# A hybrid attention layer on one core: where eight row-sum pieces, a fifth tile, halved branch loads and an FFN copy stand in the order

## The chip, the cores and the metric

The kernel runs on one core of a Trainium2 chip. A core has TensorE (PE, matmuls and transposes), VectorE (DVE), ScalarE (ACT), GpSimd (POOL) and SyncE (SP), which here only issues DMAs. Each engine works through its own queue in order. The metric is the time of one execution in device microseconds, the median of several runs.

## The reference

One encoder layer on 1024 tokens of width 1024, float32:

```python
h = rms_norm(x, norm_mix)
q_a,k_a,v_a, q_b,k_b,v_b, g_a,g_b = split(h @ w_in)
o_a = neighbourhood_attention(rms_norm(q_a), rms_norm(k_a), v_a, rpb)   # 8 heads of 64
o_b = sliding_window_attention(rms_norm(q_b), rms_norm(k_b), v_b, sink, t5)  # 8 heads, 2 kv heads
y = sigmoid(g_a) * (o_a @ w_branch_a) + sigmoid(g_b) * (o_b @ w_branch_b)
x = x + y @ w_out
h = rms_norm(x, norm_ffn)
x = x + (silu(h @ w_gate) * (h @ w_up)) @ w_down          # hidden width 2816
```

## The kernel before

**Numbers in two parts.** Every float32 operand of a large product is held as a high part (a cast) and a low part (what the cast left out); a product is three matmuls, high x high, high x low, low x high. The helper `split` does this everywhere: its cast on ACT has line L61 (L64 with a scale), its subtraction on DVE line L62 (L65 with a scale). In names, `h` and `l` behind a weight (`wb10h`, `wb10l`) are these parts, `ph` and `pl` those of a transposed tile of probabilities. The large products after the attention combine 2 x 2 blocks in seven products instead of eight; they need sums of blocks of weights (L863, class `Seven`) and of blocks of token rows (`row_sums`, class `TokenSums`).

**Order.** The PE's order is written out by hand. DVE, ACT, POOL and SP have an order that a scheduler makes from dependences, priorities and program order; `tc.issue_after(ins)` keeps what is issued inside it behind `ins`, and in the FFN's first part ACT and DVE are scheduled by hand (`change`).

**Attention.** Six head groups (`gi` 0 to 5, kind `na` or `sw`) are projected by `projection`. Each of eight token tiles gives a bank `pj` (24 matmuls, L328). Then `squares` takes the row norms of q and k (a square on ACT, the reduction L339 on DVE, an addition L343 and a power L347 on POOL), `values_out` writes the values (L368 on DVE), `scalings` applies the norms (L375). After tiles 3 and 7 `layout` transposes keys and queries in blocks: keys into a bank `tk`, scaled into `k` (L294 and L295), queries into `tq` (transposes L301, scaled by L280). `keys` and `pair` go through `both`. The tile after tile 3 is the fifth, tile 4, and its squares and values come while the first blocks of keys and queries are still in work.

The scores of a head go block by block (`scores`): two matmuls (L640, L641) into `s`, then DVE adds the bias and takes the minimum (L646), ACT takes the exponential (L652), DVE the reciprocal (L653), POOL multiplies (L654). Three steps later `flip` transposes the tiles (L664, into `tp`) and splits them (`ph`, `pl`), two steps later `values` multiplies by the values (L698). Between these, `filler` feeds PE other work at a planned rate: the projections of later groups, then gate products (`plain_gate`, L465 to L467, scaled on DVE by L491). During the gate products the row sums of the later stage are made: `row_sums` is a generator of eight pieces per index j, for the lines L539 and L540 (t1), a split (put 5), L544 (t2), put 6, L548 (t3), put 7, L552 (t4) and put 4. In `step`, piece n of j = 0 is issued at product step 26 + n, of j = 1 at 40 + n, each behind the last bound instruction (`att["bound"]`, a score sum L646 or a low half `pl`).

**Gates and branches.** Then `gate_pair` (d = 2 to 7) runs the seven products of the gate weights, into banks X, Y, V and Z (L881 to L883); it adds banks (L946, L950) and scales them (L930) on their way to DRAM. `prefetch` loads what comes two steps on, weights or, from d = 8, `load_branch`: one DMA of 128 x 1024 for the two branches' weights (`wb0s` for d = 0), then a split of each half behind the chain of earlier splits (`in_chain`). PE's product `bankX` (weights `g_1l` of gate 7) follows in that chain. The branch products then use the weights and the stored gates (`sg`).

**FFN.** After the output product the FFN's first two hidden blocks (generators `ga`, `gb`) take their seven products in the order `LAST2`; a bank is copied by L885 and L1409 on ACT, fed operands come from `feed`, weights from `prepare_ffn`, sums of weights from `add_up_ffn`. `ffn_norm` makes the second norm: transposes L1277, a reduction L1279 and a scaling L1280 on DVE, a power L1281 on POOL; `spread_norm` spreads it with transposes (L169).

Of the kernel before, what the change touches and what calls it, by code (L numbers as in the profile page):

```python
# [36 lines left out]
def block_kernel(ctx, tc, x, xt, small, w_qkv, w_gates, rpb, t5, w_branch, w_out, w_gate, w_up, w_down,  # L37
# [160 lines left out]
    class GroupWeights:  # L198
# [13 lines left out]

        def split(self, k):
            hi, lo = w_hi(f"wg{self.gi}_{k}"), w_lo(f"wg{self.gi}_{k}")
            split(hi[:, :384], lo[:, :384], self.st[k // 2][:, k % 2, :], nc.gpsimd if k % 2 and self.gi > 1 else nc.vector)
            self.his.append(hi)
            self.los.append(lo)

# [19 lines left out]
    def projection(gi, weights, pending, after=None):  # L238
# [17 lines left out]
        def both(parts):  # L256

            if gi:
                for part in parts:
                    part()()  # L260
            else:
                for low in [part() for part in parts]:
                    low()
# [67 lines left out]
        def squares(tiles):  # L331

            n, t0 = len(tiles), tiles[0][0]
            ss = ap.tile([P, 16], F32, tag="ss", name=f"ss{gi}_{t0}", bufs=4)[:, :n * nh]
            norms = ss.rearrange("p (t h) -> p t h", h=nh)
            for i, (t, ps) in enumerate(tiles):
                qn = ap.tile([P, 320], F32, tag="qn", name=f"qn{gi}_{t}", bufs=7)
                nc.scalar.activation(qn[:, :nqk], ps[:, :nqk], AF.Square)
                nc.vector.tensor_reduce(norms[:, i], qn[:, :nqk].rearrange("p (h e) -> p h e", e=HD),  # L339
                                        axis=AX.X, op=ALU.add)  # L340
                qns.append(qn)
            if n == 1:
                nc.gpsimd.tensor_scalar(ss, ss, 1.0, rows_eps[:, t0:t0 + 1], op0=ALU.mult, op1=ALU.add)  # L343
            else:
                nc.gpsimd.tensor_tensor(norms, norms, rows_eps[:, t0:t0 + n].unsqueeze(2).to_broadcast([P, n, nh]),
                                        ALU.add)
            nc.gpsimd.tensor_tensor(ss, ss, mhalf[:, :n * nh], ALU.pow)  # L347
            return tiles, norms

        def values_out(tiles):  # L350

            for t, ps in tiles:
                rs = rows_rs[:, t:t + 1]
                if kind == "na":
                    for j in range(nk):
                        nc.scalar.activation(v[j][:, t, 0, :], ps[:, nqk + j * HD:nqk + j * HD + HD], AF.Copy, scale=rs)
                else:
                    vs = ap.tile([P, HD], F32, tag="vs", name=f"vs{gi}_{t}", bufs=2)
                    nc.scalar.activation(vs, ps[:, nqk:384], AF.Copy, scale=rs)
                    dst = vnat[idx * T + t * 8:idx * T + t * 8 + 1, :]  # L360
                    nc.sync.dma_start(bass.AP(dst.tensor, dst.offset, [[64 * HD, 16], [HD, 8], [1, HD]]), vs)
                    if t == 7:
                        vr = slot_v(f"vr{gi}")[:, :512].rearrange("p (b e) -> p b e", e=HD)
                        nc.sync.dma_start(vr, vnat[idx * T:(idx + 1) * T, :].rearrange("(b p) e -> p b e", p=P))
                        late_v.append(vr)
            for t, ps in tiles if kind == "na" else ():
                for j in range(nk):
                    nc.vector.scalar_tensor_tensor(v[j][:, t, 1, :], ps[:, nqk + j * HD:nqk + j * HD + HD],  # L368
                                                   rows_rs[:, t:t + 1], f(v[j][:, t, 0, :]),
                                                   op0=ALU.mult, op1=ALU.subtract)  # L370

        def scalings(tiles, norms):

# [107 lines left out]
    def plain_gate(d, br, wg, step=None, room=()):  # L481

        for half in range(2):
# [7 lines left out]
            nc.vector.tensor_mul(raw, pg, wide_rs[half])  # L491
            nc.sync.dma_start(gate_rows(d, br, half), raw)

    def filler(pending):
        for gi in range(1, len(order)):
            for i, cost in enumerate(projection(gi, weights[gi], pending, weights.get(gi + 1))):
                if gi == len(order) - 1 and i == 58:
                    wg = gate_weights(1, 0)
                yield cost
        todo = [(0, 1), (1, 1), (0, 0), (1, 0)]  # L500
        for i, (d, br) in enumerate(todo[:3]):
            def step(half, k):
                if i == 0 and not half and k in (1, 4):
                    wide_norm(k // 4, bank("pj", f"wide{k}"))
                if (i, half, k) == (1, 0, 0):
                    load_pair(0, slot_v, dma)
                at_step = 16 * i + 8 * half + k
                if at_step == 32:
                    load_pair(1, slot_v, dma)
                if at_step in range(26, 34) or at_step in range(40, 48):  # L510
                    if at_step in (26, 40):
                        j = at_step // 40
                        g22 = early.setdefault("g22", slot_u("g22h") if not j else None)
                        early[j] = row_sums(j, halves(g22)[j])
                    with tc.issue_after(att["bound"]):
                        next(early[at_step // 40])
                if (half, k) == (0, 7):
                    step.next = gate_weights(*todo[i + 1][::-1])
                if (half, k) in ((0, 6), (1, 3), (2, 1)):
                    pop(pending)  # L520
            yield from plain_gate(d, br, wg, step)
            wg = step.next
        last_gate.append(wg)
# [46 lines left out]
    with tc.tile_pool(name="at", bufs=1) as ap:  # L570
# [165 lines left out]
        for j in range(4):  # L736
            load_x(1, j)
        for k in range(8):
            if k % 2:
                weights[0].split(k)  # L740
                feature(k, 0)
            else:
                feature(k, 0)
                weights[0].split(k)
# [26 lines left out]
        for g in range(n + LP):  # L771
            before = plan[g - 1] if g else due[0]
            if g < n:
                hd, qb = steps[g]
                while hd["gi"] not in ready:
                    fill(done_chunks[1] + 1)
                if g == 0:
                    opening.close()
                scores(hd, qb)
                if qb == 1 and g + 8 < n:  # L780
                    load_bias(steps[g + 8][0])
                if qb == (4 if g + 16 >= n else 6) and g + 8 - qb < n:
                    steps[g + 8 - qb][0]["bias"] = bias_table(steps[g + 8 - qb][0])
# [217 lines left out]

    def load_branch(d):
        st = w_stage(f"wb{d}")
        dma(st, w_branch[tok(d), :])
        for br in (1, 0):
            hi, lo = w_hi(f"wb{br}{d}"), w_lo(f"wb{br}{d}")
            in_chain(hi, lo, st[:, half_cols(br)])
# [434 lines left out]
    for i, g in enumerate((ga, gb)):  # L1442
        prepare_ffn((i, 7))
        next(g)
    add_up_ffn(4)
    feed(*((3, j) for j in range(4)))
    for i, g in enumerate((ga, gb)):
        prepare_ffn((i, 3))
        next(g)
    rs = [ffn_norm(half, sets[half]["V"]) for half in range(2)]  # L1450
    feed(*((4, j) for j in range(4)))
    both_blocks()
    prepare_ffn((0, 2), (1, 2))
# [153 lines left out]
```

## Time and profile before

| what | value |
|---|---|
| median of 3 runs | 1306.93 us (1306.88 to 1307.44) |
| the profiled execution | 1306.69 us |
| its span, first to last instruction | 1304.8 us |
| granted TensorE clock | 1.00 |
| instructions | 19431 |
| DMA packets | 88582, 191.91 MB |

The profile gives for each engine when an instruction began, how long it took and what it waited for. A timeline row has the start and length in us, the engine, the line, the operation, the tiles (out<-in), their shape and type, the count, and in brackets the idle time before it with its releaser. A wait row has the engine, its line, what it waited for, us in total, times, and the longest. A window row has the stretch, its length, then the busy time of PE, PEld (weight load), DVE, ACT and POOL with the count of instructions, the granted clock, the busy share of the DMA engines and the GB/s that they moved.

### The profile page before, as it was taken

What the parts mean: (1) busy time and instruction counts of PE and PEld (TensorE: products, weight loads), DVE (VectorE), ACT (ScalarE), POOL (GpSimd) and SP (SyncE); (2) the same over time, 40 slices, a digit from 0 to 9 for tenths busy, and PEclk for the clock granted to TensorE, in tenths of its full rate; (3) what the DMA queues carried; (4) which work ended last, traced back from release to release, by engine and by line L of the source; (5) the groups of instructions that cost most, each with busy time, mean ns of one, the idle gap of its engine ahead of it and who ended that gap; (6) DMA issues with size and microseconds to landing.
All of it is one profiled execution on the core that took longest, in us unless ns stands there. A gap on an engine that the chain in (4) does not pass through costs nothing.

```text
span 1304.8 us, 19431 instructions
## 1 busy us (share of the span) xinstructions
PE 1296.7 (99%) x6583; PEld 1129.2 (87%) x6583; DVE 1017.5 (78%) x2028; ACT 693.9 (53%) x1460; POOL 181.1 (14%) x321
## 2 busy tenths in 40 slices
PE   9999999999999999999999999999999999999998
PEld 9999999999888888888888888888888888888887
DVE  6778867776678758869899878888777799797774
ACT  7677857776654224545556544443444465363531
POOL 1355655464310000000000000000000000000000
PEclk9999999999999999999999999999999999999999
DMA  9432413242434348555763433223323356671532
GB/s 354 108 106 49 121 50 109 62 136 84 140 130 169 114 161 297 195 211 201 261 241 126 154 105 121 105 89 106 105 89 113 122 193 209 248 237 65 188 127 81
DMA packets 88582, 191.91 MB, mean 147 GB/s; under 512 B 16114, under 2 KB 18418, under 8 KB 88482
## 3 DMA queue, kind: packets, MB, share of 16 engines
q1 hardware_dynamic: 88338, 190.65, 43.6%
q8 instruction: 52, 0.85, 0.3%
q14 instruction: 48, 0.39, 0.1%
q10 hardware_dynamic: 144, 0.01, 0.0%
HBM read 133.19 MB, written 52.37 MB: 142 GB/s over the span
## 4 chain that ended last, share of the span: by engine, by line
PE 94%; DVE 2%; POOL 1%; DMA 1%; ACT 1%; issue 1%; SPq 0%; POOLq 0%; ACTq 0%; DVEq 0%
PE pj L328 14%; PE bankZ L881 6%; PE bankZ L882 6%; PE bankZ L883 6%; PE bankY L881 6%; PE bankY L882 6%; PE bankY L883 6%; PE bankX L883 5%; PE bankX L881 5%; PE bankX L882 4%; PE o L698 3%; PE bankV L881 3%; PE bankV L882 3%; PE bankV L883 3%; PE tp L664 3%; PE pb L465 2%
## 5 line engine op out<-in xcount | busy, mean ns | idle before, releaser
L652 ACT ACTIVATE E<-E,nm 128x384 f32<-128x384 f32 (+3 forms) x128 | 75.7, 592 | 49.5 <-DVE nm L646 43.9
L654 POOL TENSOR_SCALAR E<-E,nm 128x384 f32<-128x384 f32 (+1 forms) x128 | 73.4, 574 | 93.1 <-DVE nm L653 73.5
L62 DVE TENSOR_TENSOR pl<-tp,ph 128x384 fp32r<-128x384 f32 (+1 forms) x128 | 66.4, 519 | 18.2 <-ACT ph L61 17.3
L61 ACT CAST ph<-tp 128x384 fp32r<-128x384 f32 (+1 forms) x128 | 57.4, 448 | 21.5 <-PE tp L664 21.0
L61 ACT CAST f<-f 128x512 fp32r<-128x512 f32 x87 | 50.9, 621 | 27.9 <-DMA f<-u_dram 27.6
L62 DVE TENSOR_TENSOR f<-f 128x512 fp32r<-128x512 f32 x87 | 56.2, 685 | 9.5 <-ACT f L61 9.4
L664 PE MATMUL tp<-ident,E 128*128 128x128 f32 x352 | 59.6, 272 | 0.9 <-POOL E L654 0.9
L664 PEld LDWEIGHTS tp<-ident,E 128*128 128x128 f32 x352 | 45.2, 140 | 5.8 <-POOL E L654 1.2
L347 POOL TENSOR_TENSOR ss<-ss,mhalf 128x4 f32<-128x4 f32 (+2 forms) x42 | 49.7, 1183 | 3.0
L698 PE MATMUL o<-pl,v 128*128 128x256 f32 (+2 forms) x160 | 48.9, 306 | 0.5 <-DVE pl L62 0.2
L653 DVE RECIPROCAL nm<-nm 128x1 f32<-128x1 f32 x128 | 20.4, 160 | 37.1 <-ACT E L652 35.9
L1281 POOL TENSOR_TENSOR rs<-rs,mhalf 128x4 f32<-128x4 f32 x2 | 2.2, 1106 | 317.7 <-DVE rs L1280 317.7
L640 PE MATMUL s<-k,q 128*128 128x384 f32 (+1 forms) x128 | 46.0, 359 | 0.0
L698 PE MATMUL o<-ph,v 128*128 128x256 f32 (+2 forms) x160 | 45.8, 300 | 0.0
L641 PE MATMUL s<-k,q 128*128 128x384 f32 (+1 forms) x128 | 41.3, 323 | 0.0
L646 DVE CUSTOM_DVE_ANT_0 E<-s,bsw,cols 128x384 f32<-128x384 f32 (+1 forms) x64 | 37.0, 578 | 5.0 <-PE s L641 4.1
L1291 ACT ACTIVATE u<-u 128x512 f32<-128x512 f32 x44 | 27.5, 629 | 23.0 <-DVE u L1290 21.9
L646 DVE CUSTOM_DVE_ANT_0 E<-s,bna 128x384 f32<-128x384 f32 (+1 forms) x64 | 32.9, 517 | 3.3 <-PE s L641 2.7
L881 PE MATMUL bankZ<-f,f_7h 128*128 128x512 f32 x88 | 34.3, 390 | 0.1
L881 PE MATMUL bankY<-f,f_6h 128*128 128x512 f32 x88 | 34.5, 392 | 0.0
L882 PE MATMUL bankV<-f,f_5h 128*128 128x512 f32 x88 | 34.4, 391 | 0.0
L881 PE MATMUL bankV<-f,f_5h 128*128 128x512 f32 x88 | 34.4, 391 | 0.0
(1256 smaller groups left out, 4608.3 us busy)
## 6 DMA issues: line engine op xcount, KB each, us to landing
f<-u_dram SPq DMA_DIRECT2D x77, 256.0 KB
wg_s<-in_w_gate_dram SPq DMA_DIRECT2D x22, 512.0 KB
u_dram<-u SPq DMA_DIRECT2D x33, 256.0 KB
o_dram<-of SPq DMA_DIRECT2D x32, 256.0 KB
o<-o_dram SPq DMA_DIRECT2D x32, 256.0 KB
sg<-g_dram SPq DMA_DIRECT2D x32, 256.0 KB
g_dram<-go SPq DMA_DIRECT2D x24, 256.0 KB
u_dram<-tau SPq DMA_DIRECT2D x22, 256.0 KB
```

Source lines behind the costliest of these rows:

```text
L61: a = nc.scalar.copy(hi, src)
L62: b = (eng or nc.vector).tensor_tensor(lo, src, f(hi), ALU.subtract)
L328: nc.tensor.matmul(ps[:, :384], (lh, lh, ll)[n], (his, los, his)[n][k][:, :384], start=(k == 0 and n == 0), stop=(k == 7 and n == 2))
L347: nc.gpsimd.tensor_tensor(ss, ss, mhalf[:, :n * nh], ALU.pow)
L646: att["bound"] = nc.vector.tensor_tensor_reduce(E[:, :n], s[:, :n], hd["bias"](qb), -1.0, sk if sw else 1e30, ALU.add, ALU.min, nm[:, 0:1] ...
L652: nc.scalar.activation(E[:, :m], E[:, :m], AF.Exp, bias=nm[:, 0:1], scale=-1.0, accum_out=nm[:, 1:2])
L654: nc.gpsimd.tensor_scalar(E[:, :n], E[:, :n], nm[:, 1:2], 1.0, op0=ALU.mult, op1=ALU.mult)
L664: nc.tensor.transpose(tp[:, tok(j)], hd["E"][qq][:, ko:ko + P], ident)
L698: nc.tensor.matmul(hd["O"][half][:, (a - half * 4) * P:(z + 1 - half * 4) * P], v[:, kb].rearrange("p a e -> p (a e)"), pp[:, (a - q0) * P ...
L881: nc.tensor.matmul(ps, hi[:, tok(j)], bh, start=first, stop=False, skip_group_check=True)
L882: nc.tensor.matmul(ps, hi[:, tok(j)], bl, start=False, stop=False, skip_group_check=True)
L883: nc.tensor.matmul(ps, lo[:, tok(j)], bh, start=False, stop=end, skip_group_check=True)
```

## The change

It has five parts; the computation and the order of PE's matmuls stay.

1. At the start the first weight tile `wg_0` is split on DVE alone, ahead of the first feature tile.
2. In `na` groups (from the second group on) `squares` and `values_out` of tile 4 are issued behind the last split of the key and query blocks issued so far (`att["split"]`).
3. The pieces of the row sums of j = 0 leave the product steps 26 to 33. They go into a list, and `sum_piece`, called behind each `scores`, issues one. What is left is issued when the pieces of j = 1 begin.
4. A branch's load is two DMAs of 128 x 512, that for branch 1 first.
5. In the FFN `ga` goes one product further ahead of the next operands, `gb` follows after the first two of them, and the norm is taken ahead of the other two and of the weights 3.

```diff
@@ split, class GroupWeights
-            split(hi[:, :384], lo[:, :384], self.st[k // 2][:, k % 2, :], nc.gpsimd if k % 2 and self.gi > 1 else nc.vector)
+            src = self.st[k // 2][:, k % 2, :]
+            if self.gi == k == 0:
+                nc.vector.tensor_copy(hi[:, :384], src)
+                nc.vector.tensor_tensor(lo[:, :384], src, f(hi[:, :384]), ALU.subtract)
+            else:
+                split(hi[:, :384], lo[:, :384], src, nc.gpsimd if k % 2 and self.gi > 1 else nc.vector)
@@ both
-                    part()()
+                    att["split"] = part()().ins
@@ squares
+            behind = ExitStack()
+            if n == 1 and t0 == 4 and kind == "na":
+                behind.enter_context(tc.issue_after(att["split"]))
...
+            behind.close()
@@ values_out
+            behind = ExitStack()
+            if len(tiles) == 1 and tiles[0][0] == 4 and kind == "na":
+                behind.enter_context(tc.issue_after(att["split"]))
...
+            behind.close()
@@ ahead of filler
+    row_pieces = []
+
+    def sum_piece():
+        if row_pieces:
+            with tc.issue_after(att["bound"]):
+                next(row_pieces.pop())
@@ step
-                    with tc.issue_after(att["bound"]):
-                        next(early[at_step // 40])
+                    if at_step < 40:
+                        row_pieces.append(early[0])
+                    else:
+                        while row_pieces:
+                            sum_piece()
+                        with tc.issue_after(att["bound"]):
+                            next(early[1])
@@ the start
-            if k % 2:
+            if k % 2 or not k:
                 weights[0].split(k)
                 feature(k, 0)
@@ the loop over steps
                 scores(hd, qb)
+                sum_piece()
@@ load_branch
-        dma(st, w_branch[tok(d), :])
+        for br in (1, 0):
+            dma(st[:, half_cols(br)], w_branch[tok(d), half_cols(br)])
@@ the FFN's first two blocks
         next(g)
+    next(ga)
     add_up_ffn(4)
-    feed(*((3, j) for j in range(4)))
-    for i, g in enumerate((ga, gb)):
-        prepare_ffn((i, 3))
-        next(g)
+    feed((3, 0), (3, 1))
+    next(gb)
     rs = [ffn_norm(half, sets[half]["V"]) for half in range(2)]
+    feed((3, 2), (3, 3))
+    prepare_ffn((0, 3), (1, 3))
```

How this moves instructions is seen at three places. Line numbers in the changed kernel are higher: L300 is the L295 of before, L347 the L339, L380 the L368, L671 the L646, L678 the L653, L504 the L491, L577 the L552, L956 the L930, L972 the L946, L976 the L950, L889 the L863.

DVE in the sixth group, from the score sum E_0_5 on (k_1 is the second key scaling, ss_4 the reduction of the fifth tile, v_0 and v_1 its values), before:

```order
L646 ISA E_0_5_4470,nm_0_5_4471<-s_0_5_4467,bna_4021 128x384
L646 ISA nm_0_5_4471 128x1
L339 TENSOR_REDUCE ss_4_4476<-qn_4_4477 128x4
L368 SCALAR_TENSOR_TENSOR v_0_3965<-pj_4_4398,rows_rs,v_0_3965 128x64
L368 SCALAR_TENSOR_TENSOR v_1_3966<-pj_4_4398,rows_rs,v_1_3966 128x64
L295 SCALAR_TENSOR_TENSOR k_1_3968<-tk_0_4443,cols,k_1_3968 64x512
L653 RECIPROCAL nm_0_5_4471<-nm_0_5_4471 128x1
```

And in the changed kernel:

```order
L671 ISA E_0_5_4470,nm_0_5_4471<-s_0_5_4467,bna_4021 128x384
L671 ISA nm_0_5_4471 128x1
L300 SCALAR_TENSOR_TENSOR k_1_3968<-tk_0_4443,cols,k_1_3968 64x512
L347 TENSOR_REDUCE ss_4_4476<-qn_4_4477 128x4
L380 SCALAR_TENSOR_TENSOR v_0_3965<-pj_4_4398,rows_rs,v_0_3965 128x64
L380 SCALAR_TENSOR_TENSOR v_1_3966<-pj_4_4398,rows_rs,v_1_3966 128x64
L678 RECIPROCAL nm_0_5_4471<-nm_0_5_4471 128x1
```

The key scaling now stands ahead of the fifth tile's reduction and values.

DVE between the score sums E_1_2 and E_1_3 of the last head, in the gate products (hs, ta and tb are tiles of the row-sum pieces), before:

```order
L646 ISA E_1_2_5219,nm_1_2_5220<-s_1_2_5216,bna_4968 128x384
L646 ISA nm_1_2_5220 128x1
L62 TENSOR_TENSOR hs_0_5228<-tb_5134,hs_0_5228 128x512
L491 TENSOR_TENSOR graw_1_1_5245<-pg_1_1_5092,wide_rs_109 128x512
L62 TENSOR_TENSOR wg_0l<-wg01s,wg_0h 128x512
L62 TENSOR_TENSOR pl_0_6_5213<-tp_0_6_5208,ph_0_6_5212 128x384
L62 TENSOR_TENSOR wg_1l<-wg01s,wg_1h 128x512
L653 RECIPROCAL nm_1_2_5220<-nm_1_2_5220 128x1
L62 TENSOR_TENSOR pl_0_7_5242<-tp_0_7_5238,ph_0_7_5241 128x256
L552 SCALAR_TENSOR_TENSOR tb_5134<-xo_4948,cols,ta_5133 128x512
L646 ISA E_1_3_5260,nm_1_3_5261<-s_1_3_5257,bna_4968 128x384
```

And in the changed kernel:

```order
L671 ISA E_1_2_5215,nm_1_2_5216<-s_1_2_5212,bna_4968 128x384
L671 ISA nm_1_2_5216 128x1
L62 TENSOR_TENSOR pl_0_6_5209<-tp_0_6_5204,ph_0_6_5208 128x384
L504 TENSOR_TENSOR graw_1_1_5241<-pg_1_1_5092,wide_rs_109 128x512
L62 TENSOR_TENSOR wg_0l<-wg01s,wg_0h 128x512
L62 TENSOR_TENSOR wg_1l<-wg01s,wg_1h 128x512
L62 TENSOR_TENSOR hs_0_5221<-ta_5142,hs_0_5221 128x512
L678 RECIPROCAL nm_1_2_5216<-nm_1_2_5216 128x1
L62 TENSOR_TENSOR pl_0_7_5238<-tp_0_7_5234,ph_0_7_5237 128x256
L671 ISA E_1_3_5255,nm_1_3_5256<-s_1_3_5252,bna_4968 128x384
```

Of the eight pieces seven stood ahead of E_1_3 in DVE's queue before and four do now (t1, put 5, t2, put 6, whose last row is the hs row here); ahead of the low half pl_0_6 it was six and is three, and ahead of pl_1_1, a few rows further on, eight and seven.

DVE at the first branch load (wb10 and wb00 are the halves, ga7s and g_1 gate 7's weights, go_0 a gate on its way out, s1g a weight sum), before:

```order
L930 TENSOR_TENSOR go_1_6186<-gp_6187,wide_rs_109 128x512
L950 TENSOR_TENSOR go_0_6185<-bankY_5487,gp_6187 128x512
L62 TENSOR_TENSOR wb10l<-wb0s,wb10h 128x512
L930 TENSOR_TENSOR go_0_6185<-go_0_6185,wide_rs_109 128x512
L62 TENSOR_TENSOR wb00l<-wb0s,wb00h 128x512
L62 TENSOR_TENSOR g_1l<-ga7s,g_1h 128x512
L863 TENSOR_TENSOR s1g_6125<-gb_6122 128x512
```

And in the changed kernel:

```order
L956 TENSOR_TENSOR go_1_6186<-gp_6187,wide_rs_109 128x512
L62 TENSOR_TENSOR wb10l<-wb0s,wb10h 128x512
L976 TENSOR_TENSOR go_0_6185<-bankY_5487,gp_6187 128x512
L62 TENSOR_TENSOR wb00l<-wb0s,wb00h 128x512
L62 TENSOR_TENSOR g_1l<-ga7s,g_1h 128x512
L889 TENSOR_TENSOR s1g_6125<-gb_6122 128x512
L956 TENSOR_TENSOR go_0_6185<-go_0_6185,wide_rs_109 128x512
```

The gate's sum went behind the first low half, its scaling behind `g_1l` and the weight sum. On SP each branch load is two issues in its old place.

In the FFN, ACT copies bank Y to bank Z (L885) for the first block straight behind the second copy L1409, where before four casts of operands and one of weights stood between, and for the second block behind two of those casts. DVE takes both norm sums (L1279, L1280) ahead of two of the operands' low parts and of the weights' `f_3l`, where before they stood behind all of these.

## The prediction

> **What bounds the kernel now.** The busy shares of the profile's page come first, then the answer on what TensorE (PE) waited for. A PE row's gap understates a loss, since the ends of matmuls are modelled; I count a stop by starts: the interval from one matmul's start to the next, less the interval that the same shape shows where nothing waits.
>
> ```profile
> PE 1296.7 (99%) x6583; PEld 1129.2 (87%) x6583; DVE 1017.5 (78%) x2028; ACT 693.9 (53%) x1460; POOL 181.1 (14%) x321
> ...
> PE tp L664 <- POOL E L654: 0.9, 1, 0.9
> PE tq L301 <- DVE k L295: 0.6, 1, 0.6
> ```
>
> PE is busy for 1296.7 of 1304.8 us, and neither the number nor the order of its matmuls changes. So nothing can be won but stops of PE, a few us in all, and any wait in a new place is a loss. The change touches two of the waits listed there (tp and tq, quoted) and a third that carries its releaser in its own row below (bankX); the others that I sum are too short for that list and are read from starts.
>
> **Fifth tile of a projection.** The DVE (VectorE) rows of the sixth head group, and PE's beside them:
>
> ```profile
> 305.70 0.41 DVE L339 TENSOR_REDUCE ss<-qn 128x4 f32<-128x256 f32 x1
> ...
> 306.53 0.76 DVE L295 SCALAR_TENSOR_TENSOR k<-tk,cols,k 64x512 fp32r<-64x512 f32 x1
> ...
> 305.83 0.49 PE L664 MATMUL tp<-ident,E 128*128 128x128 f32 x3
> 306.08 0.42 PE L328 MATMUL pj<-wg_3h,h 128*128 128x384 f32 x1
> 306.33 0.33 PE L328 MATMUL pj<-wg_3l,h 128*128 128x384 f32 x1
> 306.50 0.34 PE L328 MATMUL pj<-wg_3h,h 128*128 128x384 f32 x1
> 307.43 0.63 PE L301 MATMUL tq<-ident,qn 128*128 128x128 f32 x4 [0.59 <-DVE k L295]
> ```
>
> A 384-wide L328 takes 0.17 from start to start (306.33 to 306.50), so the tq transposes would begin at 306.67; they begin at 307.43: **0.76 lost**. They write a bank that the second key scaling (L295) still reads. The change puts that scaling where the reduction L339 stood, 0.83 sooner (306.53 to 305.70), which ends it at about 306.46: the stop goes, with 0.07 to spare for the signal, so a few hundredths may stay. What is moved behind it is the fifth tile's reduction, its values and POOL's (GpSimd's) norm work, some 0.8 later. At this place nothing near needs them. In the two other na groups that are held back there is no stop to win, and the same move puts POOL's power behind other work. The closest case is the fifth group:
>
> ```profile
> 243.89 1.02 POOL L347 TENSOR_TENSOR ss<-ss,mhalf 128x4 f32<-128x4 f32 x1
> ...
> 245.90 0.58 POOL L654 TENSOR_SCALAR E<-E,nm 128x384 f32<-128x384 f32 x1 [0.73 <-DVE nm L653]
> ...
> 247.47 0.49 PE L664 MATMUL tp<-ident,E 128*128 128x128 f32 x3
> ```
>
> The power may now start later and stand in front of the multiply that ran at 245.90. Worst case, it begins at 245.85: the multiply ends at 246.87 + 0.58 = 247.5, and the third transpose of that group runs at 247.47 + 2 x 0.08 = 247.6. So the cost is 0, hidden by 1.1 us between 246.48 and 247.6; if that cover goes, 0.1 to 0.3 a group. I take 0.
>
> **Row-sum pieces.** Eight DVE pieces (L540, L544, L548, L552 and the splits between) move from eight consecutive product steps to one behind each of eight scores' sums (L646). PE's three stops in that stretch, the windows around it, and DVE's and POOL's rows:
>
> ```profile
> 365.68 0.33 PE L698 MATMUL o<-ph,v 128*128 128x384 f32 x1
> 365.94 0.45 PE L698 MATMUL o<-pl,v 128*128 128x384 f32 x1
> 366.22 0.38 PE L664 MATMUL tp<-ident,E 128*128 128x128 f32 x2
> ...
> 369.80 0.38 PE L664 MATMUL tp<-ident,E 128*128 128x128 f32 x2
> 371.10 0.33 PE L664 MATMUL tp<-ident,E 128*128 128x128 f32 x1 [0.92 <-POOL E L654]
> 371.18 0.48 PE L465 MATMUL pg<-h,wg_1h 128*128 128x512 f32 x1
> ...
> 357.25:370.59 13.34, 12.83 (x73) 10.64 (x71) 13.14 (x38) 9.21 (x25) 2.34 (x6) 1.00 0.40 136
> 370.59:378.00 7.41, 6.91 (x40) 6.03 (x41) 3.98 (x13) 5.51 (x14) 2.66 (x5) 1.00 0.36 130
> ...
> 367.77 0.54 DVE L646 CUSTOM_DVE_ANT_0 E<-s,bna 128x384 f32<-128x384 f32 x1
> ...
> 366.72 0.58 POOL L654 TENSOR_SCALAR E<-E,nm 128x384 f32<-128x384 f32 x1 [3.04 <-PE tp L664]
> ...
> L552 DVE SCALAR_TENSOR_TENSOR tb<-xo,cols,ta x4: 742/748/1047, 366.8 to 410.3; 128x512 f32<-128x512 f32 x4
> ```
>
> The group of three transposes takes 1.38 from its start to the next matmul (369.80 to 371.18), where 0.25 is usual (305.83 to 306.08): **1.13 lost**. The two starts around 365.94 come 0.26 and 0.28 after the ones before, not 0.17: **0.20 lost**. In the windows (columns PE, PEld, DVE, ACT, POOL) DVE works 13.14 of 13.34 us: it is the bound there, and the eight pieces are its surplus. The third transpose waits for the sum E_1_3, which DVE begins at 367.77, 3.33 before the transpose. For no stop that sum must begin 1.13 sooner, by 366.64. Before, seven pieces stand ahead of it; in the changed order four do. Three fewer pieces, at 0.74 (the L552 minimum) each, are 2.2 us; E_1_3 can begin at about 365.6. The low half that the product at 365.94 waits for had six pieces ahead of it and has three. Against that, the pieces are still done later: seven stand ahead of the low half of pl_1_1 at 370.59, where eight did, so DVE is not later there either, and the window behind it has DVE at 3.98 of 7.41, room for the last one. Gain 1.33, bounds 0 (the surplus stays in front of PE) and 1.5 (smaller gaps near 360 go too).
>
> One row speaks against it: L552 usually takes 0.74 to 0.75, but the one at 366.8, beside POOL's multiply at 366.72, took 1.05. A piece beside a multiply costs up to 0.30 more. The Trainium skill's page "SBUF — State Buffer", section "Who interferes with whom", has a rule for it: a VectorE instruction with two SBUF inputs and a GpSimd instruction that reads SBUF exclude each other, and whichever comes second waits in full. The trace agrees in kind: 0.30 longer, where a full wait to 367.30 would have made it 0.50. By the rule, pieces set between score steps, where POOL multiplies, would each lose some, and the sum would keep 0 of this term. By the rows, two or three of eight may meet a multiply, 0.6 to 0.9 against a spare of 1.0 (366.64 less 365.6): I keep the gain and make the other case a rival.
>
> **Branch loads in halves.**
>
> ```profile
> 487.78 0.62 ACT L61 CAST wb10h<-wb0s 128x512 fp32r<-128x512 f32 x1 [4.20 <-DMA wb0s<-in_w_branch_dram]
> ...
> 488.44 0.69 DVE L62 TENSOR_TENSOR wb10l<-wb0s,wb10h 128x512 fp32r<-128x512 f32 x1 [0.29 <-ACT wb10h L61]
> ...
> 490.25 0.69 DVE L62 TENSOR_TENSOR g_1l<-ga7s,g_1h 128x512 fp32r<-128x512 f32 x1
> ...
> 490.20 0.39 PE L882 MATMUL bankX<-h,g_1h 128*128 128x512 f32 x1
> 490.99 0.50 PE L883 MATMUL bankX<-h,g_1l 128*128 128x512 f32 x1 [0.40 <-DVE g_1l L62]
> ...
> 486.50:487.30 0.80, 0.80 (x6) 0.65 (x5) 0.00 (x0) 0.00 (x0) 0.00 (x0) 1.00 0.83 330
> ...
> 491.00:690.00 199.00, 199.00 (x881) 164.81 (x882) 173.43 (x278) 107.06 (x186) 0.00 (x0) 1.00 0.67 237
> ```
>
> The 512 KB load ends at 487.78 and releases a chain: cast, low half, then DVE's queue up to g_1l, which PE wants at 490.20 + 0.24 = 490.44 and gets at 490.99, 0.74 after DVE begins it: 0.55, and about 0.10 more on the next start (as at 690.42 to 690.76 below), **0.65 lost**. At 330 GB/s (last column of the window) 256 KB take 0.8 us, so the first half lands near 487.0. Its chain keeps its steps: wb10l 0.66 after the landing, g_1l three DVE steps of 0.60 behind wb10l. In those steps the sum L950, now queued behind wb10l and its DMA wait, takes the place of the scaling L930, which goes behind g_1l: the length stays, the beginning moves. So wb10l at 487.66, L950 488.26, wb00l 488.86 (its half lands at 487.78 as the whole did, time for its cast), g_1l 489.46, and PE could go on at 490.20, 0.24 before it wants to. With no earlier landing nothing is won: bounds 0 and 0.65, and I take 0.65, since the rate has its own row here. Cost: eight more issues on SP (SyncE), with gate loads queued behind; the last row shows PE at 199.00 of 199 us from there on, so I price them at 0.
>
> **FFN's first copy and norm sums.**
>
> ```profile
> 686.66 0.58 ACT L1409 COPY p<-bankV 128x512 f32<-128x512 f32 x1
> ...
> 689.78 0.59 ACT L885 COPY bankZ<-bankY 128x512 f32<-128x512 f32 x1
> ...
> 689.27 1.03 PE L1277 MATMUL bankV<-ident,wide_rs 128*128 128x128 f32 x8
> 690.42 0.50 PE L881 MATMUL bankZ<-f,f_7h 128*128 128x512 f32 x1
> 690.76 0.40 PE L882 MATMUL bankZ<-f,f_7h 128*128 128x512 f32 x1
> 691.00 0.39 PE L883 MATMUL bankZ<-f,f_7l 128*128 128x512 f32 x1
> ...
> 694.38 2.19 POOL L1281 TENSOR_TENSOR rs<-rs,mhalf 128x4 f32<-128x4 f32 x2 [317.70 <-DVE rs L1280]
> ...
> 696.00 1.28 PE L169 MATMUL bankV<-ident,rs 128*128 128x128 f32 x8
> ```
>
> Eight transposes begin at 689.27; busy 1.03 less the tail of the last leaves the next matmul due at about 690.14. It starts at 690.42, behind the copy into bankZ: 0.28, and the next start is 0.10 late (0.34 against 0.24): **0.38 lost**. The change issues that copy straight behind the one at 686.66, three us sooner, so the stop goes. The eight L169 transposes take 1.28 where L1277's eight take 1.03: **0.25 lost** to the powers on POOL, which end at 696.57. The norm sums stand two low halves and two weight lows sooner on DVE, four times 0.6 = 2.4 us; the stop goes. f_2, f_3 and the lows of f_3's weights come later by the norm sums, two reductions and two short steps on DVE; nothing that PE waits for now reads them before the L169 transposes, so I take 0, and 0.3 as the upper bound, the size of the stops here.
>
> **The start** gives the first weights' cast from ACT (ScalarE) to DVE.
>
> ```profile
> 6.54 0.72 ACT L64 ACTIVATE h<-x,cols 128x512 fp32r<-128x512 f32 x1 [0.56 <-DMA x<-in_xt_dram]
> ```
>
> ACT idles 0.56 for the second x tile, and PE needs what comes of it: a shift of the first matmuls by the 0.5 of a cast, either way, is taken up there. 0.
>
> **Sum.** 0.76 + 1.33 + 0.65 + 0.38 + 0.25 = 3.37, say 3.4. The profiled execution took 1306.69 (span 1304.8 and 1.9 around it), so it becomes 1303.3; the median is 0.24 above that execution, so I forecast **1303.5**. What a measurement can tell from no change is 0.2%, 2.6 us: faster is below 1304.3, slower above 1309.5.
>
> **The rivals.**
> A, the forecast: all five stops go, 1303.5. Chance 0.50.
> B, the half lands less than 0.56 (0.8 less the 0.24 of spare) ahead of the whole, because rows of 2 KB move more slowly than those of 4 KB or other traffic lies between: the bankX stop stays, in part or whole. For: the 330 GB/s include a store. Against: a half cannot be last. 1303.5 + 0.65 = 1304.15. Chance 0.12, half of it below 1304.3.
> C, DVE and POOL exclude each other in the pieces' new places (the rule on the shared port would do that; its page is named above): four or more collisions at 0.30 eat the spare of 1.0, and 1.33 is not won. 1304.8. Chance 0.17.
> D, another wait stands right behind each of the three large ones (the transposes' other operands, the bank's other readers): half of 0.76 + 1.13 + 0.65 stays, 1304.8. Chance 0.11.
> E, slower than before: DVE's surplus is carried past 370. One piece behind every score sum makes each following low half late by a piece, first pl_1_1. It decides when pl_1_1, which PE does not wait for now, comes less than PE's 1.3 sooner and no slack is left of it. Then 1.33 is not won and four lows wait 0.75 each: 1303.5 + 1.33 + 3.0 = 1307.8; if all eight steps do, 1310.8. For: DVE at 13.14 of 13.34. Against: one piece fewer (0.74) ahead of pl_1_1, and 3.4 us idle behind it (7.41 less 3.98). Chance 0.10, half of it above 1309.5.
> Faster: 0.50 + 0.06 = 0.56. Slower: 0.05. Same: the rest, 0.39 (0.06 of B, C, D and half of E). The range runs from 1302.7 (A, the small gaps near 360 won too, and 0.5 for the spread of the runs shown) to 1305.7 (C and D, 1304.8, and 0.9 for their unknown parts, such as the 0.3 of the fifth tile's groups and of f_2 and f_3); E is left out.
>
> **What would show it.** Right: in the list of PE's waits tp, tq and bankX are gone; the tq transposes start 0.17 after the last L328; E_1_3's sum starts more than 1.1 ahead of where it stood relative to PE's transposes; wb10h is cast more than 0.5 before where a whole load would land; the eight L169 take about 1.03. Wrong: a new row in PE's waits, above all `o <- pl` behind 370 or `tp <- POOL E` in the fifth group (both would be E's or the power's doing), pieces of over 1.0 on DVE (C), or ACT idle for wb0s until 487.7 (B).

## The result, and the profile after

The changed kernel takes 1303.35 us (median of 8 runs, 1302.70 to 1304.54), the kernel before 1307.26 (8 runs, 1306.88 to 1308.03). The ratio is 0.9971, 95% interval 0.9960 to 0.9981: 3.9 us faster, with 2.5 to 5.2 inside the interval. The profiled execution took 1304.54 (span 1302.8), the slowest of the eight; why, comes below.

PE's waits in the changed kernel. The three that the change was about (tp, tq, bankX) are gone:

```profile
PE idle L591 <- POOL ident masks.py:199: 1.4, 1, 1.4
PE pj L333 <- ACT wg_2h L61: 0.6, 1, 0.6
PE o L723 <- DVE pl L62: 0.5, 1, 0.5
```

PE's timeline at the places of the prediction, with three more that it did not sum (10.72, 354.60 and 361.06), and DVE's row of the score sum E_1_3:

```profile
10.72 0.79 PE L333 MATMUL pj<-wg_2h,h 128*128 128x384 f32 x3 [0.57 <-ACT wg_2h L61]
...
307.38 0.34 PE L333 MATMUL pj<-wg_3h,h 128*128 128x384 f32 x1
307.60 0.63 PE L306 MATMUL tq<-ident,qn 128*128 128x128 f32 x4
...
354.60 0.44 PE L723 MATMUL o<-ph,v 128*128 128x384 f32 x1
355.53 0.44 PE L723 MATMUL o<-pl,v 128*128 128x384 f32 x1 [0.50 <-DVE pl L62]
...
361.06 0.22 PE L723 MATMUL o<-ph,v 128*128 128x128 f32 x1
361.13 0.33 PE L723 MATMUL o<-pl,v 128*128 128x128 f32 x1
...
366.21 0.33 PE L723 MATMUL o<-ph,v 128*128 128x384 f32 x1
366.39 0.34 PE L723 MATMUL o<-pl,v 128*128 128x384 f32 x1
366.56 0.38 PE L689 MATMUL tp<-ident,E 128*128 128x128 f32 x2
...
370.11 0.49 PE L689 MATMUL tp<-ident,E 128*128 128x128 f32 x3
370.35 0.48 PE L478 MATMUL pg<-h,wg_1h 128*128 128x512 f32 x1
...
366.83 0.54 DVE L671 CUSTOM_DVE_ANT_0 E<-s,bna 128x384 f32<-128x384 f32 x1
...
489.45 0.39 PE L908 MATMUL bankX<-h,g_1h 128*128 128x512 f32 x1
489.68 0.39 PE L909 MATMUL bankX<-h,g_1l 128*128 128x512 f32 x1
489.90 0.39 PE L907 MATMUL bankX<-h,g_1h 128*128 128x512 f32 x1
...
688.06 1.03 PE L1304 MATMUL bankV<-ident,wide_rs 128*128 128x128 f32 x8
688.85 0.48 PE L907 MATMUL bankZ<-f,f_7h 128*128 128x512 f32 x1
689.17 0.39 PE L908 MATMUL bankZ<-f,f_7h 128*128 128x512 f32 x1
...
694.40 1.03 PE L169 MATMUL bankV<-ident,rs 128*128 128x128 f32 x8
695.20 0.47 PE L907 MATMUL bankY<-f,f_3h 128*128 128x512 f32 x1
```

The same places of the kernel before that have not been shown:

```profile
9.52 0.97 PE L328 MATMUL pj<-wg_2h,h 128*128 128x384 f32 x4
...
354.35 0.34 PE L698 MATMUL o<-ph,v 128*128 128x384 f32 x1
354.75 0.44 PE L698 MATMUL o<-pl,v 128*128 128x384 f32 x1
...
360.27 0.22 PE L698 MATMUL o<-ph,v 128*128 128x128 f32 x1
360.59 0.33 PE L698 MATMUL o<-pl,v 128*128 128x128 f32 x1
...
697.03 0.48 PE L881 MATMUL bankY<-f,f_3h 128*128 128x512 f32 x1
```

Read from start to start, before and after:

| place | before | after | won | predicted |
|---|---|---|---|---|
| tq transposes | 0.93 | 0.22 | 0.71 | 0.76 |
| low half near 360 | 0.32 | 0.07 | 0.25 | not summed |
| two starts near 366 | 0.54 | 0.35 | 0.19 | 0.20 |
| three transposes near 371 | 1.38 | 0.24 | 1.14 | 1.13 |
| bankX, two starts | 1.13 | 0.45 | 0.68 | 0.65 |
| bankZ, two starts | 1.49 | 1.11 | 0.38 | 0.38 |
| eight L169 | 1.03 | 0.80 | 0.23 | 0.25 |
| sum | | | 3.58 | 3.37 |

The two profiled executions differ by only 2.15 us (1306.69 to 1304.54). The rest of the 3.58 was lost in this one execution at two places: the third projection group begins at 10.72, not at 9.52 (1.20), and the low half at 355.5 comes 0.93 behind the product before it, not 0.40 (0.53). Together 1.73; about 0.3 the other way are small differences elsewhere. Both places move from execution to execution, with the change and without it, as the experiments below show.

The rows of the tile xo (min, median and max in ns of the piece t4) and of the window of the row-sum pieces with the one behind it:

```profile
L577 DVE SCALAR_TENSOR_TENSOR tb<-xo,cols,ta x4: 739/742/745, 370.6 to 409.0; 128x512 f32<-128x512 f32 x4
...
357.25:370.59 13.34, 13.34 (x78) 11.73 (x78) 12.31 (x34) 9.25 (x25) 3.33 (x6) 1.00 0.44 154
370.59:378.00 7.41, 7.41 (x46) 6.35 (x44) 5.80 (x19) 6.70 (x17) 2.53 (x4) 1.00 0.34 124
```

No t4 runs slowly now. In the window where DVE had been busy for 13.14 of 13.34 us it is busy for 12.31, and PE for all of it. Two of the eight pieces (t4 and put 4) now lie in the window behind, where DVE is busy for 5.80 of 7.41 us, not 3.98, and PE for all of it too.

### The profile page after: what moved, and what is told of

Same layout as the page of the kernel before. It is cut to its first block, busy times and chain, and to the rows that moved or that the text cites. A ratio compares the mean times of both kernels' runs of the same rounds, so it can differ in the third digit from the quotient of the medians.

```text
span 1302.8 us, 19452 instructions
## 1 busy us (share of the span) xinstructions
PE 1296.1 (99%) x6583; PEld 1130.1 (87%) x6583; DVE 1016.2 (78%) x2029; ACT 694.4 (53%) x1459; POOL 180.8 (14%) x321
## 4 chain that ended last, share of the span: by engine, by line
PE 97%; DMA 1%; DVE 1%; POOL 0%; issue 0%; ACT 0%; SPq 0%
PE pj L333 15%; PE bankZ L907 6%; PE bankZ L908 6%; PE bankZ L909 6%; PE bankY L908 6%; PE bankY L909 6%; PE bankY L907 6%; PE bankX L908 5%; PE bankX L909 5%; PE bankX L907 5%; PE o L723 3%; PE bankV L908 3%; PE bankV L907 3%; PE bankV L909 3%; PE tp L689 3%; PE pb L480 2%
## 5 line engine op out<-in xcount | busy, mean ns | idle before, releaser
L678 DVE RECIPROCAL nm<-nm 128x1 f32<-128x1 f32 x128 | 20.4, 160 | 37.1 <-ACT E L677 35.9
L671 DVE CUSTOM_DVE_ANT_0 E<-s,bsw,cols 128x384 f32<-128x384 f32 (+1 forms) x64 | 36.9, 576 | 4.0 <-PE s L666 3.3
L671 DVE CUSTOM_DVE_ANT_0 E<-s,bna 128x384 f32<-128x384 f32 (+1 forms) x64 | 33.0, 517 | 2.6 <-PE s L666 2.0
L911 ACT COPY bankZ<-bankY 128x512 f32<-128x512 f32 x42 | 24.1, 575 | 19.7 <-PE bankY L909 19.7
```

The costliest lines, as they stand in the source:

```text
L671: att["bound"] = nc.vector.tensor_tensor_reduce(E[:, :n], s[:, :n], hd["bias"](qb), -1.0, sk if sw else 1e30, ALU.add, ALU.min, nm[:, 0:1] ...
```

## The experiments

All times are medians beside runs of the kernel before on the same chip. Parts are those of the change.

### Parts 2 to 5, each alone on the kernel before

**Row-sum pieces**, with the lists of `step` and one `sum_piece()` behind each `scores`:

```diff
                 scores(hd, qb)
+                sum_piece()
```

> Part 3 alone on the kernel before. If the row-sum pieces are what PE waited for near 366 and 371 and the terms add, this is 1.3 to 1.6 us faster than before: the group of three transposes near 371 takes 0.25 again, not 1.38. If VectorE's surplus is only carried on, the stop near 371 goes but others come behind it, and the time is within 0.3 us of before. The stops at tq, bankX, bankZ and at the spread transposes stay in either case.

1305.76 against 1307.36, ratio 0.9988 (0.9978 to 0.9997): 1.6 us faster. The transposes near 371 take 0.25:

```profile
369.28 0.49 PE L676 MATMUL tp<-ident,E 128*128 128x128 f32 x3
369.53 0.48 PE L465 MATMUL pg<-h,wg_1h 128*128 128x512 f32 x1
```

The gaps near 360 and 366 are gone here as well, and no wait is listed behind 371: the surplus was spread, not carried on.

**Fifth tile**, with `both`, `squares` and `values_out` as changed:

```diff
+            if n == 1 and t0 == 4 and kind == "na":
+                behind.enter_context(tc.issue_after(att["split"]))
```

> Part 2 alone. If the late second key scaling alone held the tq transposes, 0.7 us faster than before, with the tq start 0.17 to 0.25 behind the last L328 product. If the tq transposes also wait for something else, or the power of GpSimd now delays the multiplies of the third and fifth group, 0 to 0.3 us faster or slower.

1306.10 against 1307.36, ratio 0.9990 (0.9980 to 0.9999). PE's timeline:

```profile
306.99 0.34 PE L328 MATMUL pj<-wg_3h,h 128*128 128x384 f32 x1
307.20 0.41 PE L301 MATMUL tq<-ident,qn 128*128 128x128 f32 x2
```

The step is 0.21, so 0.72 was won here; the median moved by 1.3, which the interval (0.1 to 2.6 us) allows and the trace does not explain. The power on POOL delayed nothing that is listed: PE has no wait for E in the third or fifth group, and the one wait for E in its list is the stop near 371, which part 3 is about.

**Branch loads in halves.**

```diff
-        dma(st, w_branch[tok(d), :])
+        for br in (1, 0):
+            dma(st[:, half_cols(br)], w_branch[tok(d), half_cols(br)])
```

> Part 4 alone. If the landing of the first half starts the chain to g_1l sooner, the bankX stop of 0.65 us goes and wb10h is cast 0.5 us or more before where the whole load landed, relative to PE. If the order of VectorE is what matters and the halves land together, the stop stays, wb10h is cast when the whole has landed, and the time is that of before.

1306.97 against 1307.36, ratio 0.9998 (0.9988 to 1.0007): too small to be timed. The trace shows it. ACT's and PE's timelines:

```profile
487.41 0.62 ACT L61 CAST wb10h<-wb0s 128x512 fp32r<-128x512 f32 x1 [2.94 <-DMA wb0s<-in_w_branch_dram]
...
491.08 0.39 PE L882 MATMUL bankX<-h,g_1h 128*128 128x512 f32 x1
491.31 0.39 PE L883 MATMUL bankX<-h,g_1l 128*128 128x512 f32 x1
```

The stop is gone (0.23). The cast comes 3.90 ahead of the product with g_1l; in the profile of before it came at 487.78, 2.66 ahead of where PE wanted that product (490.44). One profile of each is little to go by here, since the landing moves from execution to execution. In the six profiles of kernels whose wanted half does not come first (before, the other parts alone, and the other order below), the cast is 2.7 to 2.9 ahead and the two starts lose 0.41 to 0.68. In the eight profiles where it comes first the cast is 3.6 to 3.9 ahead and nothing is lost. So the half serves 0.7 to 1.2 us sooner, which agrees with the 0.8 forecast, and the stop goes in every profile; the profile that the prediction quotes shows it at its largest.

**FFN.**

```diff
+    next(ga)
     add_up_ffn(4)
...
     rs = [ffn_norm(half, sets[half]["V"]) for half in range(2)]
+    feed((3, 2), (3, 3))
+    prepare_ffn((0, 3), (1, 3))
```

> Part 5 alone. If the copy into bankZ and the norm's powers held PE, both stops go, 0.5 to 0.6 us faster than before. If the lows moved behind the norm sums are late for the products after the spread transposes, a new stop near 697 takes up to 0.3 of it back.

1306.59 against 1307.36, ratio 0.9994 (0.9985 to 1.0004): not to be told from no change by its time. By PE's timeline both stops are gone and none is new near them (four starts near 1102 come 0.44 later in all, but with part 3 alone the same four come 0.59 later, so that is not this part's doing):

```profile
689.19 1.03 PE L1277 MATMUL bankV<-ident,wide_rs 128*128 128x128 f32 x8
689.98 0.48 PE L881 MATMUL bankZ<-f,f_7h 128*128 128x512 f32 x1
...
695.53 1.04 PE L169 MATMUL bankV<-ident,rs 128*128 128x128 f32 x8
696.32 0.47 PE L881 MATMUL bankY<-f,f_3h 128*128 128x512 f32 x1
```

The four medians add up to 1.60 + 1.26 + 0.39 + 0.77 = 4.02 us; the whole change brings 3.91. Each of these medians is uncertain by about 1.2 us, so the agreement is closer than the times can support; the traces carry it.

### The start

**Part 1 alone.**

```diff
+            if self.gi == k == 0:
+                nc.vector.tensor_copy(hi[:, :384], src)
+                nc.vector.tensor_tensor(lo[:, :384], src, f(hi[:, :384]), ALU.subtract)
```

> Part 1 alone. If the landing of the first weights and of the next x tiles sets the start, the first projection product begins within 0.1 us of what the other kernels show (about 5.05) and the time is that of before within 0.3 us. If the cast on VectorE holds up the first feature's low half, 0.3 to 0.5 us slower, with a PE wait for h at the seventh to twelfth product; if the free ScalarE serves sooner, up to 0.5 us faster.

1307.32 against 1307.35, ratio 0.9998 (0.9989 to 1.0008). In PE's timeline its first product is at 4.50, but its third group only at 10.40, as with part 2 alone, whose first product is at 5.08:

```profile
10.40 0.62 PE L333 MATMUL pj<-wg_2h,h 128*128 128x384 f32 x2 [0.33 <-ACT wg_2h L61]
```

What was expected of the first product (within 0.1 of 5.05) was wrong; that nothing comes of it held.

**The whole change without part 1**, the two edits above undone.

> The changed kernel without part 1. If part 1 does nothing, the median is that of the changed kernel within 0.3 us, the first product begins 0.4 to 0.5 us later (about 5.05), and the third product group at 9.4 to 10.8 as everywhere. If part 1 costs what the first profile of the changed kernel lost, 0.5 to 1.2 us faster than the changed kernel.

1303.62 against 1307.17, ratio 0.9976 (0.9967 to 0.9985); first product at 5.08, as expected, third group at 10.23. The median is 0.53 above that of the changed kernel beside it (next run), more than the 0.3 expected, but its eleven runs spread from 1302.60 to 1305.74.

**The changed kernel once more.**

> The changed kernel once more, as it is. Its first profile shows 1.2 us lost against that of before ahead of the fourth tile of weights, in the start that the other kernels share. If that is the spread of the first loads from run to run, the start of this profile is anywhere between the two, what follows it takes 1207.5 within 0.7 us, and the median is 1303.3 within 0.4. If the changed start costs, the third product group begins at 10.7 again.

1303.09 against 1307.17, ratio 0.9971 (0.9960 to 0.9981); the third group at 10.23, and the low half that was at 355.53 comes 0.30 behind its product here. So the 1.2 us was the first execution's. Over all profiles whose loads at the start are those of before, the third group begins at 9.52 to 10.64 without part 1 (six) and at 9.39 to 10.82 with it (seven). In all thirteen it begins 0.56 to 0.63 behind the start of the cast of wg_2h on ACT: the landing of that load sets it. The change does not decide that, and part 1 is worth nothing that these runs can tell.

The 1207.5 us of the expectation fits no stretch of these profiles that I can name. From the third group to the end of the span the two executions of the changed kernel take 1292.1 and 1291.0 us; 0.63 of the difference is the low half near 355.

### What makes the stops go

**Halves in the other order.**

```diff
-        for br in (1, 0):
+        for br in (0, 1):
             dma(st[:, half_cols(br)], w_branch[tok(d), half_cols(br)])
```

> The changed kernel with the two halves of a branch load issued in the other order, so that wb10h's half lands last. If the sooner landing of its half is what removed the bankX stop, the stop comes back (0.4 to 0.7 us) and the time is 0.4 to 0.7 above the changed kernel's. If two smaller DMAs or VectorE's new order did it, no stop and the time of the changed kernel.

1304.22 against 1307.35, ratio 0.9974 (0.9965 to 0.9984): about 0.9 us above the changed kernel, though the intervals of the two overlap. The stop is back in PE's timeline:

```profile
488.05 0.39 PE L908 MATMUL bankX<-h,g_1h 128*128 128x512 f32 x1
488.63 0.50 PE L909 MATMUL bankX<-h,g_1l 128*128 128x512 f32 x1 [0.19 <-DVE g_1l L62]
488.97 0.40 PE L907 MATMUL bankX<-h,g_1h 128*128 128x512 f32 x1
```

0.58 and 0.34, not 0.23 each: 0.46 lost, half of what the median shows. Two smaller DMAs alone do not help; the half that is wanted first must be first. With this order the scheduler also put the sum ahead of wb10l again, as before. That is not what holds the chain: by DVE's and ACT's rows the sum ends at 485.99 and the cast, which wb10l needs, at 486.05.

**A piece ahead of each score sum.**

```diff
-                scores(hd, qb)
-                sum_piece()
+                sum_piece()
+                scores(hd, qb)
```

> The changed kernel with each row-sum piece issued ahead of a score sum, not behind it. Five pieces, not four, then stand ahead of E_1_3. If the count of pieces ahead decides, two fewer than before are 1.5 us and the stop near 371 stays away (under 0.2 us): within 0.3 of the changed kernel. If the place behind the sum is what matters, each score sum is late by its piece and the stop near 371 is back with 0.7 us or more.

1304.35 against 1307.35, ratio 0.9976 (0.9966 to 0.9986), about 1 us above the changed kernel, again with overlapping intervals. DVE's, POOL's and PE's timelines:

```profile
365.57 0.21 DVE L678 RECIPROCAL nm<-nm 128x1 f32<-128x1 f32 x2
...
365.89 1.58 POOL L679 TENSOR_SCALAR E<-E,nm 128x384 f32<-128x384 f32 x2 [4.60 <-DVE nm L678]
...
365.48 0.27 PE L689 MATMUL tp<-ident,E 128*128 128x128 f32 x1
366.53 0.33 PE L689 MATMUL tp<-ident,E 128*128 128x128 f32 x1 [0.79 <-POOL E L679]
366.62 0.42 PE L665 MATMUL s<-k,q 128*128 128x384 f32 x1
```

The stop near 371 stayed away, as the count of pieces says, but one of 1.00 came a group earlier: two transposes take 1.14 to the next matmul (365.48 to 366.62), 0.14 in the changed kernel (366.56 to 366.70). The reciprocal of E_1_1 stands behind four long operations here (a gate's scaling, two weight lows and a piece, each 0.67 to 0.68), together with that of E_1_2, and POOL multiplies only at 365.89. In the changed kernel it ran on its own at 362.96. So the count alone, by which the prediction reckoned, does not decide: the place of each step's reciprocal does as well, and one piece directly behind a sum leaves it free.

### The two places left

**g22 later.** In the changed kernel's profile ACT stood 2.58 us for a load, with the exponentials queued behind:

```profile
350.44 0.72 ACT L564 ACTIVATE g22h<-xo,cols 128x512 f32<-128x512 f32 x1 [2.58 <-DMA xo<-in_xt_dram]
```

```diff
-        nc.scalar.activation(g22, b22, AF.Copy, scale=gb)
         nc.vector.tensor_tensor(t1, b12, b11, ALU.subtract)
         yield
         put(5, t1, ga)
+        nc.scalar.activation(g22, b22, AF.Copy, scale=gb)
```

> The changed kernel, with the scaled block g22 of the row sums computed on ScalarE behind the second piece, not ahead of the first. In the trace of the changed kernel ScalarE waits for the block's DMA at 350.4 us, with the exponential of E_0_3 queued behind it, and PE waits 0.7 us for a low half near 355.5. If that queueing is the cause, the wait goes: 0.2 to 0.7 us faster than the changed kernel, about 1302.9. If the block's cost is only moved, t2 and what follows come later and nothing is won.

1303.39 against 1307.35, ratio 0.9968 (0.9958 to 0.9979), 7 runs from 1302.12 to 1305.89: not to be told from the changed kernel. A second time beside it:

> The changed kernel with g22 behind the second piece, once more, beside the changed kernel on the same chip. The wait near 355.5 is 0 here and 0.2 to 0.7 us in the changed kernel, by when the block's load lands: 0.3 us faster than the changed kernel on the median, at most 0.7.

1302.71 (6 runs, 1302.44 to 1303.50) beside 1303.09 (7 runs, 1303.00 to 1303.78), ratio to before 0.9969 (0.9956 to 0.9981). PE no longer waits:

```profile
353.54 0.34 PE L723 MATMUL o<-ph,v 128*128 128x384 f32 x1
353.71 0.33 PE L723 MATMUL o<-pl,v 128*128 128x384 f32 x1
```

The stop is shown to go, and its cause with it. In the eleven profiles with g22 in its old place ACT's wait for this load goes from 1.73 to 2.60 us, and the interval between the two products from 0.17 to 0.94, in the same order: each time it is the wait less 1.6. In the three with g22 later it is 0.17 or 0.18. On the mean of the eleven the stop costs 0.37 us, about the 0.4 by which the two medians beside each other differ.

**The third group's loads in halves as well**, on the kernel with g22 later.

```diff
-        load_x(0, 1)
+        load_x(0, 1, 0)
         weights[0].load(1)
+        load_x(0, 1, 1)
...
-            for k in ((0, 1), (1, 2)) if self.gi == u == 0 else ((0, 2),):
+            for k in ((0, 1), (1, 2)) if self.gi == 0 and u < 2 else ((0, 2),):
```

> As the run before, and the second x tile's and the second weights' load at the start in halves, those for the third product group first. If that group waits for bytes (a load of 384 KB and one of 512 KB, of which it needs half), it begins 0.5 to 1.0 us sooner, at 9.0 to 9.8, and PE's wait for wg_2h goes: 0.4 to 1.0 us faster than the run before. If the time to the first landing sets it, not the bytes, or later loads wait behind two more issues, it is unchanged or a wait for wg_4h takes its place.

1302.10 (5 runs, 1301.87 to 1303.13) against 1307.17, ratio 0.9964 (0.9952 to 0.9977): the lowest median of all, 1.0 below the changed kernel and 0.6 below the run before (1302.71), which differs from it by these loads alone. The ranges of those two overlap. In its list of PE's waits only the row of `idle` shown above remains. ACT casts wg_2h sooner than in any of the thirteen profiles with whole loads (8.76 to 10.25), and by PE's timeline the third group begins with no wait ahead of it:

```profile
7.86 0.51 ACT L61 CAST wg_2h<-wg_1s 128x384 fp32r<-128x384 f32 x1 [0.25 <-DMA wg_1s<-in_w_qkv_dram]
...
9.19 0.85 PE L333 MATMUL pj<-wg_2h,h 128*128 128x384 f32 x4
```

It now stands 1.33 behind the cast, not 0.56 to 0.63, straight behind the products before it: in this profile the load no longer sets it. Part of the gain is lost again soon after, where the expectation had its rival, though for no listed wait: at the products of wg_4l (13.70) two starts come 0.29 later than in the run before. Of the 0.74 that its third group is sooner against that run's, 0.45 is left.

## Why the prediction was right, point by point

- **The sum** (1303.5, range to 1305.7): measured 1303.35. All five stops went, and in the two profiles compared each term is within 0.05 of its table row; each part alone brings its own stop's end in the trace. Left out was the gap near 360, 0.25.
- **Against what it was summed.** The working took 0.24 between the profiled execution and the median. Over eight runs it is 0.57, so the gain is 3.9, not 3.4. The quoted execution had an early third group: 9.52, where the runs with the same loads lie between 9.39 and 10.82. I took one draw for the rule. That the forecast is only 0.15 off is in part luck: the gain was 0.5 more than forecast, and the kernel before, over eight runs, 0.33 slower than the figure from which it was taken.
- **Fifth tile.** 0.76 forecast, 0.71 measured: the few hundredths that were to stay are there. The cover for the moved norm work held.
- **Row pieces.** 1.13 and 0.20 forecast, 1.14 and 0.19 measured, but the argument was only half right. Three pieces fewer were to bring E_1_3 forward by 2.2, 1.0 more than needed. It begins 3.28 ahead of the three transposes (366.83 to 370.11), where it had begun 2.03 ahead (367.77 to 369.80): 1.25 sooner, of 1.13 needed. The sum E_1_2, with two pieces fewer ahead of it, came only 0.08 sooner against the same transposes, since it stands behind the reciprocal of E_1_1, ahead of which DVE sits idle for 0.17 until ACT is done (362.96). The multiply behind E_1_3 also followed sooner (2.27 behind the sum, not 2.68) and ended 0.6 ahead of the third transpose. So the stop went with less to spare than the 1.0 against which collisions were weighed. And the run with the pieces ahead of the sums has five, and lost 1.00 elsewhere.
- **Rival C** (DVE and POOL exclude each other) did not come about: t4, at most 1047 ns before, took 739 to 745 ns in all four, since in its new place no multiply ran beside it. One piece ahead of 370 still met a multiply for more than 0.1 us: put 7 began at 369.39, 0.30 ahead of the end of the multiply of 369.10, and took 0.83, where the same operation takes 0.68 at 365.83. That is 0.15 longer, half of a full wait, and it stands behind E_1_3, so that PE did not notice. The rule of the page "SBUF — State Buffer" (the Trainium skill), section "Who interferes with whom", is thus seen in kind and not in size: by it whichever of the two comes second waits in full, and the rows, in which POOL's spans are rough, show half.
- **Rival E** (surplus carried on): DVE is busier behind 370 (5.80 of 7.41 us, not 3.98), so work was carried there, but no wait for a low half behind 370 is in PE's list: the room that the prediction saw was enough.
- **Rival D** (another wait right behind each of the large ones): none is in PE's list, and the start-to-start intervals are the usual ones.
- **Halves.** 0.65 forecast, 0.68 measured. The cost of the stop was read off one execution, the one in which it was largest; in five other profiles without the right half first it is 0.41 to 0.60. Rival B is out: the half does not land late, and with the other order the stop is back.
- **FFN.** 0.38 and 0.25 forecast, 0.38 and 0.23 measured. The 0.38 was split wrongly, and the errors cancel: the matmul behind the eight transposes was due after 0.79, not 0.87, and the next one 0.32 after it, not 0.24 (688.06, 688.85, 689.17).
- **The start.** Priced at 0, and so it is (1307.32 against 1307.35), but for another reason than I gave: not the wait for x at 6.54 but that of the third group for its weights (wg_2h) takes up the shift.

## What to carry to other kernels

Where one engine is busy for 99%, list its stops by start-to-start intervals, find for each what ended it, and a sum over them forecasts to a few tenths. Before subtracting from one profiled execution, see how far its loads at the start and its DMA-bound waits vary: here two such places moved by 1.43 and 0.77 us, more than any part of the change but one. A load of which the first consumer needs half was worth cutting here, if that half went first.

## What the runs showed of the hardware

PE ran at half speed at the start for a time that differs between executions. The two profiles of the changed kernel show it, with the same warm-up matmuls from 1.62 or 1.63 us on. In the first the four products with wg_0l took 1.35, one start every 0.32 us:

```profile
6.01 1.35 PE L333 MATMUL pj<-wg_0l,h 128*128 128x384 f32 x4
```

In the second the same four took 0.88, one start every 0.18 us:

```profile
5.56 0.88 PE L333 MATMUL pj<-wg_0l,h 128*128 128x384 f32 x4
```

The granted clock reads 1.00 in both stretches, so only the intervals tell. The Trainium skill's page "TensorE: Matmul & The Clock Gate", section "Part 1: The HAM clock gate (the "warmup" mystery)", says that TensorE starts at half its clock and is raised after a busy window of some 3.4 us, and that this window runs freely and does not begin with the kernel; the traces agree that the moment is not set by the kernel. With whole loads the half speed cost at most 0.07 us, since the third group waits for wg_2h in any case (0.56 to 0.63 behind its cast in all thirteen profiles).
